# Column weights of the input and up projections kept as pairs in five slots, each starting at another byte offset modulo 512

## The chip, the cores and the metric

The kernel runs on one core of one Trainium2 chip. The metric is the device time of one execution in microseconds; lower is better. "TensorE", "VectorE", "ScalarE", "GpSimd" and "SyncE" are the core's engines; the profile calls them PE, DVE, ACT, POOL and SP, and lists TensorE's weight loads apart as PEld. SBUF is the on-chip memory with 128 partitions, PSUM holds the matmul results in 8 banks, DRAM is off-chip memory.

## The reference

One decoder layer over a sequence of 2048 positions with 1024 channels, in float32. Its parts, cut to what is computed:

```python
h = rms_norm(x, mix_norm_g[l])
z = h @ w_in[l]                                  # 1024 -> 2048: the input projection
lru_x, lru_gate, conf_a, conf_b = jnp.split(z, [D_LRU, 2 * D_LRU, 2 * D_LRU + D_CONF], axis=-1)
lru_x = causal_dwconv(lru_x, lru_conv_w[l], lru_conv_b[l])              # 4 taps
y_lru = rg_lru(lru_x, ...) * jax.nn.gelu(lru_gate, approximate=True)
c = conf_a * jax.nn.sigmoid(conf_b)
c = causal_dwconv(c, conf_conv_w[l], conf_conv_b[l])                    # 31 taps
c = jax.nn.silu(layer_norm(c, conf_ln_g[l], conf_ln_b[l]))
x = x + jnp.concatenate([y_lru, c], axis=-1) @ w_out[l]
...
x = x + o @ w_o[l]                               # cross-attention into 256 memory tokens
h = rms_norm(x, ffn_norm_g[l])
g, u = jnp.split(h @ w_up[l], 2, axis=-1)        # 1024 -> 6144: the up projection
g = causal_dwconv(g, ffn_conv_w[l], ffn_conv_b[l])                      # 3 taps
x = x + (jax.nn.gelu(g, approximate=True) * u) @ w_down[l]              # 3072 -> 1024
return rms_norm(x, final_norm_g)
```

## The kernel before

The kernel first records all its operations in a `Program`, and a planner then decides their order on each engine before anything is emitted. All operations are emitted in one place (line 394), so the profile tells them apart by tile names and not by lines.

**Precision.** A float32 product is made of three float32r products (TensorE's rounded float32): each operand is split into a high part, a rounded copy made by ScalarE, and a low part, source minus high part, made by VectorE (`split`, line 566). `mm3` then issues high x high, high x low and low x high into the same PSUM bank. The first operand of a matmul is the stationary one, 128x128, loaded into TensorE ahead of the matmul; the second one moves through it, mostly 512 columns wide.

**The two projections.** In the input projection (`project`) and the up projection (`strassen_cols`) the weights are the stationary operand. They come in blocks of 4 x 128 rows by 128 columns, each split into a high and a low tile of 128 x 512 elements, named wh and wl and made by `pair("w", (P, KQ, P))`. One such pair serves 12 matmuls: four 128-row steps, three products each.

- The input projection runs once per quarter of the sequence (four "mixers" of 512 positions). In the first mixer the weights are loaded raw, split, used, and stored to DRAM as w_in2 (`Columns.store`); the three later mixers load the stored parts again (`Columns.get`, `Kept.get`), 32 pairs each.
- The up projection runs once per half of the sequence, in 12 chunks of 256 gate and 256 value columns. Each of these column blocks is computed by Strassen's method with seven products per block pair; sums of raw blocks (tiles named s) are made by VectorE, split, and used once. That makes 2 x 12 x 2 x 7 = 336 pairs. The moving operands are seven sets of four split tiles (Xh, Xl), 56 tiles that stay in SBUF for a half. The tiles u, up, gb and cv take the PSUM results, their sums and the convolution with its gelu.
- While the up projection runs, `prepare_down` splits the combined blocks of w_down, also with pairs named wh and wl, but without the shape argument, and stores them for the down projection, where they are the moving operand.

**Slots.** Every working tile is one of a class: S (128 x 512, 84 slots), W (raw weights, 128 x 1024, 4 slots), D (128 x 1152, 3 slots) and ps (8 PSUM banks). Within a class the planner hands slots out strictly in the order in which the program created the tiles; a slot is free when the last operation on its tile has ended. S, W and D slots are 2048, 4096 and 4608 bytes per partition, all multiples of 512, and the first of them starts on a multiple of 512. The constants (identity matrix, ones) lie 128 bytes past one.

**Order.** `deadlines` gives each operation a due time, counted back from the order of TensorE's work, also through the slots (the operation that frees a slot is due before the one that needs it). `schedule` lets each engine take its ready operation with the nearest due time. The result is a fixed instruction order per engine; an instruction whose operands are not there holds up those behind it on its engine. All DMAs are issued by SyncE, in one such order. Stores have a slack of 30 us in their due times.

Of the kernel before, what the change touches and what calls it, by code (L numbers as in the profile page):

```python
# [12 lines left out]
F32R = mybir.dt.float32r  # L13
# [4 lines left out]
P = 128  # L18
S = 2048
D = 1024  # L20
NK = D // P
KQ = NK // 2
TT = 512
NQ = S // TT
NH = NQ // 2
NTB = TT // P
# [12 lines left out]

SLOTS = dict(S=84, W=4, D=3, ps=8)
WIDTH = dict(S=TT, W=1024, D=1152, ps=TT)


ACT_SETS = {AF.Exp: (0,), AF.Tanh: (0, 2, 11, 18), AF.Sigmoid: (2,), AF.Sqrt: (3,),
# [84 lines left out]
class Program:  # L131
# [3 lines left out]
    def __init__(self, nc, place):  # L135

        self.nc, self.place = nc, place
        self.ops, self.clock, self.group, self.queues = [], 0.0, None, {t: [] for t in SLOTS}
        self.first = False
        self.engines = dict(PE=nc.tensor, DVE=nc.vector, ACT=nc.scalar, Pool=nc.gpsimd, SP=nc.sync)  # L140

    def new(self, tag, shape=None, dtype=F32, name="t"):
        b = Buf(tag, shape or (P, WIDTH[tag]), None, dtype, name)
        self.queues[tag].append(b)
        return b
# [68 lines left out]
    def prepare(self):  # L214

        for tag, queue in self.queues.items():
            live = []
            for b in queue:
                while live and live[0] < b.ops[0].idx:
                    heapq.heappop(live)  # L220
                heapq.heappush(live, b.ops[-1].idx)
                assert len(live) <= SLOTS[tag], tag
        for o in self.ops:
# [3 lines left out]
        for tag, queue in self.queues.items():  # L227
            dead = sorted(queue, key=lambda b: b.ops[-1].idx)
            for i, b in enumerate(queue[SLOTS[tag]:]):
                for u in dead[i].ops:  # L230
# [24 lines left out]
    def schedule(self):  # L255
# [3 lines left out]
        idle = {e: True for e in self.engines}  # L259
        free = {t: list(range(n)) for t, n in SLOTS.items()}  # L260
        queues = {t: list(reversed(q)) for t, q in self.queues.items()}
# [13 lines left out]
        def grant(tag, t):  # L275
            while free[tag] and queues[tag]:
                b = queues[tag].pop()
                b.slot = free[tag].pop(0)
                b.left = len(b.ops)
                for o in b.heads:  # L280
                    satisfied(o, t)
# [62 lines left out]
        for tag, queue in self.queues.items():  # L344
            for b in queue:
                for o in b.heads:
                    o.wait += 1
        for tag in SLOTS:
            grant(tag, 0.0)
# [68 lines left out]
def hybrid_layer(  # L418
# [12 lines left out]

    def place(b, slot):
        pool = psp if b.tag == "ps" else spool
        return pool.tile([P, WIDTH[b.tag]], b.dtype, name=b.name, tag=f"{b.tag}{slot}", bufs=1)

    pr = Program(nc, place)

    def const(shape, name, dtype=F32):
        return Buf(None, shape, cpool.tile(list(shape), dtype, name=name), dtype, name)

    def V(name, *a, **k):
        pr.do("DVE", name, *a, **k)
# [20 lines left out]
    def tmp(name="tmp"):  # L463
        return pr.new("S", name=name)

    def rnd(name, shape=None):
        return pr.new("S", shape, F32R, name)

    def pair(name, shape=None):
        return rnd(name + "h", shape), rnd(name + "l", shape)  # L470


# [93 lines left out]
    def split(src, hi, lo):  # L566
        ACT(hi[:], src, AF.Copy)
        V("tensor_tensor", lo[:], src, hi[:].f32(), op=ALU.subtract)
# [13 lines left out]
    def load_gates():  # L582
        for name, w in (("gwa", lru_w_a), ("gwx", lru_w_x)):
            g = tmp()
            V("memset", g[:], 0.0)
            gr = g[:].split2(NC4)
            wr = w[0].rearrange("(c t) i j -> t i c j", t=2)
            for t in range(2):
                pr.dma(gr[t * 64 : t * 64 + 64, :, t * 64 : t * 64 + 64], wr[t])
            hi, lo = pair(name)  # L590
            split(g[:], hi, lo)
            gates.append((hi, lo))


    class Kept:
# [12 lines left out]
            self.tok[i] = Buf(None, (1,))  # L608
            pr.dma(self.at(i), src.f32(), writes=[self.tok[i]])

        def get(self, i, shape=None, name=None):
            b = pr.new("S", shape, self.dtype, name or self.name)
            pr.dma((b[:] if shape is None else flat(b)).f32(), self.at(i), reads=[self.tok[i]])
            return b

    def raw_cols(w, c0, kq):
        st = pr.new("W", (P, KQ, 2 * P), name="raw")
        pr.dma(st[:], w[kq * KQ * P : (kq + 1) * KQ * P, c0 : c0 + 2 * P].rearrange("(k p) f -> p k f", p=P))
        return st
# [6 lines left out]
    def split_cols(st, f):  # L626
        hi, lo = pair("w", (P, KQ, P))
        split(st[:, :, f * P : (f + 1) * P], hi, lo)
        return hi, lo

    def flat(b):
        return Ref(b, (lambda ap: ap.rearrange("p k f -> p (k f)"),), np.broadcast_to(np.int8(0), (P, TT)))

    class Columns:

# [5 lines left out]
        def get(self, c0, kq):  # L641
            key = (c0, kq)
            n = self.seen[key] = self.seen.get(key, 0) + 1
            base = ((c0 // (2 * P)) * 2 + kq) * 4
            if n > 1:
                return [tuple(self.kept.get(base + 2 * f + i, (P, KQ, P), "w" + "hl"[i]) for i in range(2)) for f in range(2)]
            st = self.early.pop(key, None) or raw_cols(self.w, c0, kq)
            got = self.rounded(c0, kq, st)
            if n < self.uses:
                self.store(c0, kq, got)  # L650
            return got
# [8 lines left out]
        def store(self, c0, kq, got):  # L660
            base = ((c0 // (2 * P)) * 2 + kq) * 4
            for f in range(2):
                for i in range(2):
                    self.kept.put(base + 2 * f + i, flat(got[f][i]))

    class Rows:
# [5 lines left out]
        def get(self, k, half):  # L672
            base = (k * 2 + half) * 2
            n = self.seen[k, half] = self.seen.get((k, half), 0) + 1
            if n > 1 or self.w is None:
                return tuple(self.kept.get(base + i, None, "w" + "hl"[i]) for i in range(2))
            st = tmp("raw")
            pr.dma(st[:], self.w[k * P : (k + 1) * P, half * TT : (half + 1) * TT])
            hi, lo = pair("w")
            split(st[:], hi, lo)  # L680
            if n < self.uses:
                self.kept.put(base, hi[:])
                self.kept.put(base + 1, lo[:])
            return hi, lo
# [38 lines left out]
    class Stats:  # L723
# [3 lines left out]
        def add(self, tb, half, src):  # L727
            i = half * NTB + tb
            ACT(junk[:], src, AF.Square, accum_out=self.ss[:, i : i + 1])
# [313 lines left out]
    x2_kept = Kept("x2", NQ * NTB * 2, F32)  # L1043
# [131 lines left out]
    def attend(q, ready):  # L1175
# [7 lines left out]
        def add(tb, half, p):  # L1183
            V("tensor_tensor", xs[tb][half][:], xs[tb][half][:], p[:], op=ALU.add)
            st.add(tb, half, xs[tb][half][:])

        yield from project_tokens(L + Y, W_out, add, None, ATT_PACE[q][0])
        del L, Y
        r = st.rstd()
# [232 lines left out]
    wd_kept = Kept("w_down2", NCK * 7 * KD * 2)  # L1422

    def wd_at(c, key, i):
        return ((c * 7 + ORDER.index(key)) * KD + i) * 2
# [29 lines left out]
    class Down:  # L1455
# [34 lines left out]
        def gather(self, c, n):  # L1490
            if (c, n) in self.ready:
                return self.ready.pop((c, n))
            akey, bkey = self.STEPS[n]
            L, R = [], []
            for i in range(KD):
                src = self.operand(c, akey, i)
                hi, lo = pair("hid")
                split(src[:], hi, lo)
                L.append((hi, lo))
                at = wd_at(c, bkey, i)  # L1500
                R.append(self.given[c, n][i] if (c, n) in self.given else (wd_kept.get(at, None, "wh"), wd_kept.get(at + 1, None, "wl")))
            self.R = R
            return L, R

# [13 lines left out]
        def add(self, banks, th, half):  # L1518
            for tb in range(NTB):
                at = (th, tb, half)  # L1520
                if at not in self.acc:
                    self.acc[at] = x2_kept.get(((2 * self.h + th) * NTB + tb) * 2 + half, None, "acc")
                t = self.acc[at]
                V("tensor_tensor", t[:], t[:], banks[tb][:], op=ALU.add)

# [110 lines left out]
    m, n, a = mixers, normeds, attends  # L1636
# [40 lines left out]
```

## Time and profile before

| | us |
|---|---|
| median of two timed runs | 2470.62 (2469.7 to 2471.55) |
| the profiled execution | 2470.41 |
| its span, first to last instruction | 2468.5 |
| TensorE busy in the span | 2450.5 |
| VectorE busy | 1825.8 |
| ScalarE busy | 1171.0 |

The stages follow each other roughly so: mixers with the preparation of the attention weights and the first attention quarters until about 800 us, the remaining attention until 1070 us, the up projection until about 2010 us, the down projection to the end. DMA moved 543.70 MB in the span, 220 GB/s in the mean.

How to read the rows that the prediction quotes: in rows of instruction groups stand line, engine, operation, output tile and input tiles with the buffer numbers left out, rows and columns, and shape, then the count; after the bar the group's busy time, the mean nanoseconds of one, and how long the engine sat idle before them, with what ended that. Rows of waits give who waited for whom, the total, the number and the longest, in us. Rows of windows give the stretch, its length, then each engine's busy time with its number of instructions in the order TensorE, weight loads, VectorE, ScalarE, GpSimd, then the granted clock, the DMA engines' busy share and GB/s. Rows of the timeline give start, duration, engine and instruction; equal ones that follow each other are merged with a count. Matmuls overlap in the pipeline, so a matmul's listed duration is longer than the distance to the next one.

### The profile page before, as it was taken

How to read it: one execution, taken by the hardware profiler on the slowest of the kernel's cores; microseconds unless marked ns; L12 is line 12 of the kernel's file. 1: busy time of each engine (PE TensorE's matmuls, PEld its weight loads, DVE VectorE, ACT ScalarE, POOL GpSimd, SP SyncE). 2: the span in 40 equal slices, each digit the busy share in tenths (PEclk: the TensorE clock that was granted, in tenths of full speed). 3: DMA queues.
4: the chain of work that ended last, by engine and by line, in shares of the span. 5: the costliest groups of instructions: out<-in, count | busy, mean ns of one | idle time of the engine just before them, and what ended most of it. 6: DMA issues, size and time to landing. Idle time of an engine off the chain costs nothing. (4 is left out here: it accounts for less than half of the span.)

```text
span 2468.5 us, 32772 instructions
## 1 busy us (share of the span) xinstructions
PE 2450.5 (99%) x11212; PEld 2037.8 (83%) x11212; DVE 1825.8 (74%) x3041; ACT 1171.0 (47%) x2041; POOL 0.7 (0%) x6
## 2 busy tenths in 40 slices
PE   9999999999999999999999999999999999999998
PEld 7898888888888788888888888888888888888887
DVE  7999993697279532369888887987886675667666
ACT  6762664366416543465545455555454432224223
POOL 0000000000000000000000000000000000000000
PEclk9999999999999999999999999999999999999999
DMA  9598676677456748777654545444542387779675
GB/s 318 209 302 320 214 256 236 214 257 257 150 174 238 250 158 293 260 254 249 234 196 151 181 165 178 166 165 163 179 145 94 120 279 263 247 253 357 234 253 177
DMA packets 327741, 543.70 MB, mean 220 GB/s; under 512 B 31580, under 2 KB 109404, under 8 KB 327574
## 3 DMA queue, kind: packets, MB, share of 16 engines
q1 hardware_dynamic: 327574, 541.60, 63.9%
q8 instruction: 89, 1.46, 0.2%
q14 instruction: 78, 0.64, 0.1%
HBM read 396.78 MB, written 144.70 MB: 219 GB/s over the span
## 5 line engine op out<-in xcount | busy, mean ns | idle before, releaser
L394 PE MATMUL ps<-Xh,wh 128*128 128x512 f32 x1344 | 523.4, 389 | 0.0
L394 PE MATMUL ps<-Xh,wl 128*128 128x512 f32 x1344 | 523.0, 389 | 0.1
L394 PE MATMUL ps<-Xl,wh 128*128 128x512 f32 x1344 | 522.9, 389 | 0.0
L394 DVE SCALAR_TENSOR_TENSOR conv<-cb,v,conv 128x512 f32<-128x512 f32 x480 | 339.6, 743 | 2.8 <-ACT conv L394 0.9
L394 PEld LDWEIGHTS ps<-Xh,wl 128*128 128x128 f32 x1344 | 252.2, 188 | 53.2 <-DVE wl L394 0.6
L394 PEld LDWEIGHTS ps<-Xh,wh 128*128 128x128 f32 x1344 | 252.3, 188 | 52.7 <-DVE up L394 0.4
L394 PEld LDWEIGHTS ps<-Xl,wh 128*128 128x128 f32 x1344 | 252.3, 188 | 52.2
L394 PE MATMUL ps<-wl,hidh 128*128 128x512 f32 x672 | 261.4, 389 | 0.0
L394 PE MATMUL ps<-wh,hidh 128*128 128x512 f32 x672 | 261.4, 389 | 0.0
L394 PE MATMUL ps<-wh,hidl 128*128 128x512 f32 x672 | 261.4, 389 | 0.0
L394 DVE TENSOR_TENSOR acc<-acc,ps 128x512 f32<-128x512 f32 x192 | 129.4, 684 | 143.8 <-PE ps L394 141.2
L394 PE MATMUL ps<-xh,wh 128*128 128x512 f32 x512 | 202.7, 396 | 0.8 <-ACT xt L394 0.8
L394 PE MATMUL ps<-xh,wl 128*128 128x512 f32 x512 | 199.4, 389 | 0.0
L394 PE MATMUL ps<-xl,wh 128*128 128x512 f32 x512 | 199.3, 389 | 0.0
L394 ACT ACTIVATE wh<-s 128x512 fp32r<-128x512 f32 x192 | 119.3, 627 | 111.9 <-DVE s L394 85.6
L394 ACT ACTIVATE wh<-raw 128x512 fp32r<-128x512 f32 x208 | 127.1, 626 | 85.0 <-PE ps L394 40.1
L394 DVE TENSOR_TENSOR wl<-raw,wh 128x512 fp32r<-128x512 f32 x208 | 141.0, 684 | 24.6 <-ACT wh L394 22.9
L394 DVE TENSOR_TENSOR wl<-s,wh 128x512 fp32r<-128x512 f32 x192 | 131.1, 686 | 29.0 <-ACT wh L394 20.2
L394 ACT ACTIVATE u<-ps 128x512 f32<-128x512 f32 x144 | 85.9, 597 | 138.9 <-PE ps L394 137.9
L394 PEld LDWEIGHTS ps<-wh,hidh 128*128 128x128 f32 x672 | 126.1, 188 | 26.2
L394 PEld LDWEIGHTS ps<-wl,hidh 128*128 128x128 f32 x672 | 126.1, 188 | 26.2
L394 PEld LDWEIGHTS ps<-wh,hidl 128*128 128x128 f32 x672 | 126.1, 188 | 26.1
(206 smaller groups left out, 4246.0 us busy)
## 6 DMA issues: line engine op xcount, KB each, us to landing
raw<-in_w_up_dram SPq DMA_DIRECT2D x96, 512.0 KB
wh<-w_down SPq DMA_DIRECT2D x164, 256.0 KB
wl<-w_down SPq DMA_DIRECT2D x164, 256.0 KB
wh<-w_in SPq DMA_DIRECT2D x96, 256.0 KB
wl<-w_in SPq DMA_DIRECT2D x96, 256.0 KB
hid<-cv SPq DMA_DIRECT2D x48, 512.0 KB
h<-hid SPq DMA_DIRECT2D x96, 256.0 KB
w_down<-wh SPq DMA_DIRECT2D x84, 256.0 KB
```

The costliest lines, as they stand in the source:

```text
L394: getattr(e, name)(*[resolve(a) for a in args], **{k: resolve(a) for k, a in kw.items()})
```

## The change

Pairs with a shape argument, that is the column weights of the input and up projections, get a class T of their own: one tile of 128 x 1024 elements with the high part in its first half and the low part in its second. T has five slots of 4608 bytes per partition (1024 + 128 elements of 4 bytes). Within slot n the pair starts `T_AT[n]` elements from the slot's start: 0, 192, 64, 128 and 32 bytes for the slots 0 to 4. The class S goes from 84 to 74 slots. `Kept.get_pair` loads the two stored parts with two DMAs into the halves of one T tile; `join` marks the second as not waiting for the first. The other hunks of the diff only drop an argument from the calls of `Kept.get`.

```diff
-SLOTS = dict(S=84, W=4, D=3, ps=8)
-WIDTH = dict(S=TT, W=1024, D=1152, ps=TT)
+SLOTS = dict(S=74, T=5, W=4, D=3, ps=8)
+WIDTH = dict(S=TT, T=1024, W=1024, D=1152, ps=TT)
+T_PAD, T_AT = 128, [0, 48, 16, 32, 8]
...
     def place(b, slot):
         pool = psp if b.tag == "ps" else spool
+        if b.tag == "T":
+            t = pool.tile([P, WIDTH["T"] + T_PAD], b.dtype, name=b.name, tag=f"T{slot}", bufs=1)
+            return t[:, T_AT[slot] : T_AT[slot] + WIDTH["T"]]
         return pool.tile([P, WIDTH[b.tag]], b.dtype, name=b.name, tag=f"{b.tag}{slot}", bufs=1)
...
     def pair(name, shape=None):
+        if shape is not None:
+            t = pr.new("T", (P, 2 * KQ, P), F32R, name)
+            return t[:, :KQ], t[:, KQ:]
         return rnd(name + "h", shape), rnd(name + "l", shape)
...
-        def get(self, i, shape=None, name=None):
-            b = pr.new("S", shape, self.dtype, name or self.name)
-            pr.dma((b[:] if shape is None else flat(b)).f32(), self.at(i), reads=[self.tok[i]])
+        def get(self, i, name=None):
+            b = pr.new("S", None, self.dtype, name or self.name)
+            pr.dma(b[:].f32(), self.at(i), reads=[self.tok[i]])
             return b
+
+        def get_pair(self, i, name):
+            got = pair(name, (P, KQ, P))
+            for n, b in enumerate(got):
+                pr.dma(flat(b).f32(), self.at(i + n), reads=[self.tok[i + n]], join=n > 0)
+            return got
...
     def flat(b):
-        return Ref(b, (lambda ap: ap.rearrange("p k f -> p (k f)"),), np.broadcast_to(np.int8(0), (P, TT)))
+        return Ref(b.buf, b.steps + (lambda ap: ap.rearrange("p k f -> p (k f)"),), np.broadcast_to(np.int8(0), (P, TT)))
...
             if n > 1:
-                return [tuple(self.kept.get(base + 2 * f + i, (P, KQ, P), "w" + "hl"[i]) for i in range(2)) for f in range(2)]
+                return [self.kept.get_pair(base + 2 * f, "w") for f in range(2)]
```

More of the change, by code (lines that the diff above doesn't have):

```diff
@@ L675, in get @@
             if n > 1 or self.w is None:
-                return tuple(self.kept.get(base + i, None, "w" + "hl"[i]) for i in range(2))
+                return tuple(self.kept.get(base + i, "w" + "hl"[i]) for i in range(2))
             st = tmp("raw")
@@ L1500, in gather @@
                 at = wd_at(c, bkey, i)
-                R.append(self.given[c, n][i] if (c, n) in self.given else (wd_kept.get(at, None, "wh"), wd_kept.get(at + 1, None, "wl")))
+                R.append(self.given[c, n][i] if (c, n) in self.given else (wd_kept.get(at, "wh"), wd_kept.get(at + 1, "wl")))
             self.R = R
@@ L1521, in add @@
                 if at not in self.acc:
-                    self.acc[at] = x2_kept.get(((2 * self.h + th) * NTB + tb) * 2 + half, None, "acc")
+                    self.acc[at] = x2_kept.get(((2 * self.h + th) * NTB + tb) * 2 + half, "acc")
                 t = self.acc[at]
```

## The prediction

> **What bounds the kernel now.** I read the page first, then instructions grouped by line and shape, then the waits, then busy time by windows.
>
> ```profile
> span 2468.5 us, 32772 instructions
> PE 2450.5 (99%) x11212; PEld 2037.8 (83%) x11212; DVE 1825.8 (74%) x3041; ACT 1171.0 (47%) x2041; POOL 0.7 (0%) x6
> PEclk9999999999999999999999999999999999999999
> ```
>
> TensorE is busy from end to end at the full granted clock. The profiled execution took 2470.41 us (1.91 us around its span), the two timed runs have a median of 2470.62; the sum below is made against 2470.4. "Busy" alone could hide gaps, because each matmul is listed longer than the distance to the next. So I look at what TensorE waited for, largest first, and the last of the ten rows:
>
> ```profile
> PE ps L394 <- DMA raw<-in_ffn_norm_g_dram: 3.3, 1, 3.3
> PE ps L394 <- ACT mem L394: 2.0, 1, 2.0
> PE ps L394 <- DVE sum L394: 1.7, 1, 1.7
> ...
> PE ps L394 <- DVE xl L394: 0.3, 1, 0.3
> ```
>
> Nothing of note. Hence the time is the number of matmuls times the distance between them, and only two things can move it: that distance, or new waits. The distance comes from a window that holds nothing but 512-column matmuls of the up projection:
>
> ```profile
> 1600.00:2000.00 400.00, 400.00 (x1766) 331.23 (x1765) 305.85 (x463) 188.03 (x286) 0.00 (x0) 1.00 0.43 147
> ```
>
> 400/1766 = 226.5 ns each, although one is listed at 389 ns and its weight load at 188 ns in the rows that follow. What does the distance consist of? The matmuls of 256 columns tell, also in rounded float32 (float32r), each with a fresh 128x128 weight load:
>
> ```profile
> 128.70 0.28 PE L394 MATMUL ps<-kvl,qth 128*128 128x256 f32 x1
> ...
> 130.38 0.28 PE L394 MATMUL ps<-kvh,qth 128*128 128x256 f32 x1
> ```
>
> These are 14 steps in 1.68 us, 120 ns each. So 256 more columns cost 106.5 ns (0.416 ns a column), and 120 - 256 x 0.416 = 13.5 ns remain per matmul, whatever its length. This constant is the only thing that the byte shift can remove.
>
> **What the shift touches.** The matmuls whose stationary operand moves into the new slots are these six groups, three of the up and three of the input projection:
>
> ```profile
> L394 PE MATMUL ps<-Xh,wh 128*128 128x512 f32 x1344 | 523.4, 389 | 0.0
> L394 PE MATMUL ps<-Xh,wl 128*128 128x512 f32 x1344 | 523.0, 389 | 0.1
> L394 PE MATMUL ps<-Xl,wh 128*128 128x512 f32 x1344 | 522.9, 389 | 0.0
> L394 PE MATMUL ps<-xh,wh 128*128 128x512 f32 x512 | 202.7, 396 | 0.8 <-ACT xt L394 0.8
> L394 PE MATMUL ps<-xh,wl 128*128 128x512 f32 x512 | 199.4, 389 | 0.0
> L394 PE MATMUL ps<-xl,wh 128*128 128x512 f32 x512 | 199.3, 389 | 0.0
> ```
>
> 3 x (1344 + 512) = 5568 matmuls, 12 to a pair, so 464 pairs. By the changed program's order the unshifted slot serves 95 of them; 369 pairs, 4428 matmuls, read their weights 32, 64, 128 or 192 bytes off. Every slot of the old program holds a multiple of 512 bytes, and weights and moving operand of all its float32r matmuls start at the same place modulo 512. So no row of before shows a float32r matmul with a shift. Bounds: at best the whole constant goes, 4428 x 13.5 ns = 59.8 us. At worst I have no row; the weight load may grow from 188 ns by 38 ns before it reaches the distance of 226.5.
>
> Which value? The nearest rows are plain float32. The identity matrix starts 128 bytes off a multiple of 512, the tile x on one:
>
> ```profile
> 7.56 1.91 PE L394 MATMUL ps<-ident,x 128*128 128x128 f32 x16
> 9.30 1.91 PE L394 MATMUL ps<-ident 128*128 128x128 f32 x16
> ```
>
> Sixteen transposes with operands 128 bytes apart and sixteen of the identity with itself (no distance at all) take the same 1.91 us. The weight load shows no price either: in `sum,ones` the stationary matrix lies 128 bytes off, in `mt,raw` on a multiple:
>
> ```profile
> L394 PEld LDWEIGHTS ps<-mt,raw 128*128 128x128 f32 x256 | 48.3, 190 | 8.2 <-DVE al L394 1.2 <-issue 0.5
> L394 PEld LDWEIGHTS ps<-sum,ones 128*128 128x128 f32 x16 | 3.0, 190 | 2.7 <-DVE sum L394 2.1
> L394 PEld LDWEIGHTS ps<-Xl,wh 128*128 128x128 f32 x1344 | 252.3, 188 | 52.2
> ```
>
> 190 and 190 ns. I take 0 for the shift, gain and loss, and keep the ends. A second reason against a clash of two reads: once one stream has been held up by a step it no longer meets the other, so a clash should not return for every load with the same 13.5 ns at 256 and 512 columns. A constant does. The Trainium skill (TensorE: Matmul & The Clock Gate, "Step-by-step: what each phase is for") states that TensorE has two independent read ports, one for the moving operand and one for weight loads, so that a load takes no read bandwidth from the running matmul. By that rule the shift is worth nothing, and the sum stays as it is. The same page's "Back-to-back issue gap" gives 2.5 ns above the column time for a warm matmul. The trace shows 13.5 ns for float32r, so the page's figure does not hold here, and what fills the difference is open.
>
> **What the slots cost.** Before, a pair took any two of 84 general slots; now it needs one of five. A slot is free when the last of its 12 matmuls has run and, in the first mixer, when both its stores to DRAM have landed. With five slots in turn, a refill has four products of time: 4 x 12 x 226.5 ns = 10.9 us. The refill itself is one copy and one subtraction:
>
> ```profile
> L394 ACT ACTIVATE wh<-s 128x512 fp32r<-128x512 f32 x192 | 119.3, 627 | 111.9 <-DVE s L394 85.6
> L394 DVE TENSOR_TENSOR wl<-s,wh 128x512 fp32r<-128x512 f32 x192 | 131.1, 686 | 29.0 <-ACT wh L394 20.2
> ```
>
> 0.63 + 0.69 = 1.3 us, which leaves 9.6 us for what stands ahead in the two queues. Behind a refill that waits for its slot stand ScalarE's PSUM copies (u) and VectorE's additions into gb and up, for which TensorE's banks wait. The longest single instructions there are:
>
> ```profile
> L394 DVE SCALAR_TENSOR_TENSOR cv<-gb,v,cv 128x1024 f32<-128x1024 f32 x40 | 51.2, 1280 | 5.3 <-ACT cv L394 3.4 <-DMA wd<-in_w_down_dram 1.3
> L394 DVE TENSOR_TENSOR cv<-cv,up 128x512 f32<-128x512 f32 x40 | 27.4, 685 | 0.4
> L394 ACT ACTIVATE cv<-gb,v 128x1024 f32<-128x1024 f32 x20 | 24.8, 1238 | 14.9 <-DVE gb L394 14.7
> ```
>
> In the changed order nine of the 459 refills have less time: two come one product after the release (2.7 us), seven two products (5.4 us). One instruction ahead in each queue makes a refill 1.3 + 1.24 + 1.28 = 3.8 us: the two are late by 1.1 us each, the seven are not. Price 2 us, between 0 and 10 us if all nine were late by that much.
>
> The first mixer splits 32 pairs and stores each (0.52 MB):
>
> ```profile
> 0.00:100.00 100.00, 94.70 (x461) 79.96 (x462) 81.60 (x169) 68.28 (x121) 0.70 (x6) 1.00 0.87 304
> 700.00:800.00 100.00, 99.16 (x453) 82.02 (x452) 99.54 (x169) 44.39 (x68) 0.00 (x0) 1.00 0.59 202
> ```
>
> At 304 GB/s a pair's store takes 1.7 us, within refill distances of 9.7 to 14 us there. DMA engines are 87% busy, so some will land late: I take 2 us, up to 13 if each of 26 refills is late by 0.5. The later mixers load 96 pairs by DMA; the tightest stretch is at 737 to 750 us with 10.9 us from release to use, and at 202 GB/s (the row above) 0.52 MB takes 2.6 us. These two DMAs now wait at SP for TensorE's release, with x, xn and w_out loads behind them. SP waits in this way already:
>
> ```profile
> SPq L394 <- PE ps L394: 623.2, 330, 30.1
> ```
>
> No TensorE wait came of it, so 0. The number and size of DMAs stay the same. The 74 general slots hold 56 tiles of split activations during the up projection, which leaves 18 instead of 28, but the ten are those that the pairs used: 0. The down projection gets ten slots less and none back; its program-order peak is 56 of 74: 0.
>
> Sum: 2470.4 + 0 (shift) + 2 + 2 = 2474.4, so 2474.
>
> **Rivals.**
>
> The shift works (faster). If the 13.5 ns are two reads at the same place modulo 512, the four shifted slots lose it in whole or in part: 2474.4 - 59.8 = 2415 in whole, and about 2456 if three tenths go. For it: the constant is there, and all float32r operands do start at the same place. Against it: the transposes above, and a constant independent of length. Chance 0.12 in all, 0.03 of it for the 83% of the constant that make 2%.
>
> VectorE's burst empties the five slots (slower). Its place is the convolution of each of 24 chunks in the up projection: four cv steps and four products, 4 x 1.28 + 4 x 0.685 = 7.9 us of VectorE. Run in one piece, that is under the 9.6 us of cover; it decides from 9.6 on. Two additions into gb (0.69 each) and two s sums on top make 10.7, late by 1.1 us a chunk; with two more of each, 13.4, late by 3.8. Over 24 chunks that is 26 to 91 us; at 2.4 late it is 58 us, 2532. For it: VectorE was 93% busy at 1100 to 1200 us and 89% at 1500 to 1600:
>
> ```profile
> 1100.00:1200.00 100.00, 99.84 (x449) 82.07 (x448) 92.91 (x151) 59.77 (x94) 0.00 (x0) 1.00 0.71 245
> 1500.00:1600.00 100.00, 100.00 (x443) 82.81 (x442) 88.96 (x143) 56.42 (x92) 0.00 (x0) 1.00 0.52 179
> ```
>
> Against it: the planner puts the instruction with the nearest due time first, a split before a convolution step, and between 1600 and 2000 us VectorE has 94 of 400 us to spare. Chance 0.06.
>
> The shift hurts: each nanosecond of distance costs 4.4 us, 11 of them 2%. Nothing shows it; chance 0.02. That the change doesn't do what it says is excluded: a slot is 4608 bytes, nine times 512, so the starts do differ as written.
>
> **How the numbers follow.** Forecast 2474, chance 0.80, between 2468 and 2494 by the bounds above (10 and 13 us of lateness at the upper end). The range takes in a small relief down to 2458 (2.8 ns of the constant, 12 us off 2470.4). Left out are most of the relief case (0.10) and the two slow ones (0.08). About 2% can be told from no change, 49 us: faster 0.03, slower 0.05 (the burst beyond 49 us, and the shift's own price), the rest within.
>
> **What would show it.** Matmuls per microsecond in a window of the up projection: still 4.4 if the shift does nothing, up to 4.7 if it removes the constant. In the same window TensorE's distance would differ from pair to pair, by slot. TensorE's waits on wl (now w) growing from under 1 us to a few says that the slots cost what I priced; tens of microseconds there, at chunk boundaries, is the burst. I am wrong if the distance moves in either direction, or if waits appear outside the nine short refills and the first 100 us.

## The result and the profile after

The changed kernel takes 2505.18 us (median of two runs, 2504.64 to 2505.71), the one before 2470.62: a ratio of 1.014 with a 95% interval of 1.0096 to 1.0183. It is 34.6 us slower, outside the predicted range of 2458 to 2494, and by more than the runs scatter. The profiled execution took 2504.64 us with a span of 2502.9, which is 34.4 more than before. All operations now stand at line 395, as the diff adds a line above.

The page's head after, with busy time and count of each engine:

```profile
span 2502.9 us, 32672 instructions
PE 2479.1 (99%) x11212; PEld 2038.9 (81%) x11212; DVE 1829.3 (73%) x3041; ACT 1177.1 (47%) x2044; POOL 0.7 (0%) x6
PEclk9999999999999999999999999999999999999999
```

The count of matmuls, the time of all weight loads (2037.8 before) and the granted clock are all but the same, and TensorE is still busy from end to end. Its busy time grew by 28.6 us. The same window of the up projection as in the prediction:

```profile
1600.00:2000.00 400.00, 400.00 (x1728) 324.25 (x1727) 311.25 (x471) 187.36 (x284) 0.00 (x0) 1.00 0.41 142
```

1728 matmuls where 1766 were: 400/1728 = 231.5 ns from one to the next instead of 226.5, at full clock and without a gap. Does the whole kernel run slower, or only what reads the new slots? The groups by form after, in the columns of the prediction, first those with a pair, then those of the down projection, which uses none, then a weight load from a pair:

```profile
L395 PE MATMUL ps<-Xh,w 128*128 128x512 f32 x2688 | 841.4, 394 | 2.7 <-DVE w L395 0.9 <-ACT u L395 0.7 <-ACT Xh L395 0.6
L395 PE MATMUL ps<-Xl,w 128*128 128x512 f32 x1344 | 528.7, 393 | 0.2 <-DVE Xl L395 0.2
L395 PE MATMUL ps<-wh,hidh 128*128 128x512 f32 x672 | 261.5, 389 | 0.8 <-ACT hidh L395 0.8
L395 PE MATMUL ps<-wl,hidh 128*128 128x512 f32 x672 | 261.4, 389 | 0.0
...
L395 PEld LDWEIGHTS ps<-Xh,w 128*128 128x128 f32 x2688 | 504.7, 188 | 121.3 <-DVE w L395 1.9 <-ACT u L395 1.3 <-ACT Xh L395 1.0
```

Of these rows only the matmuls with a pair are longer (394 and 393 against 389 ns); the loads from it are listed at 188 ns as before. So what slows are the matmuls, and the load's own row doesn't show it. The waits of TensorE, largest first, are the smaller part:

```profile
PE ps L395 <- DMA raw<-in_ffn_norm_g_dram: 3.5, 1, 3.5
PE ps L395 <- ACT xt L395: 2.2, 2, 1.3
PE ps L395 <- ACT xh L395: 1.7, 1, 1.7
...
PE ps L395 <- DVE w L395: 0.9, 1, 0.9
```

The 34.4 us can be divided by the distances between the starts of successive matmuls in the two traces, each put beside the 226.75 ns (120 ns at 256 columns) of the kernel before. Steps that touch a shifted operand are longer by 23.5 us in sum (4530 steps), steps just behind them and other unshifted ones by 1.7 more than before, gaps (what steps of 300 ns and more have above that distance) grew from 12.0 to 22.1 us, and the rest is 0.9 us less.

### The profile page after: what moved, and what is told of

It reads as the page before. It is cut to its first block, busy times and chain, and to the rows that moved or that the text cites. A ratio compares the mean times of both kernels' runs of the same rounds, so it can differ in the third digit from the quotient of the medians.

```text
span 2502.9 us, 32672 instructions
## 1 busy us (share of the span) xinstructions
PE 2479.1 (99%) x11212; PEld 2038.9 (81%) x11212; DVE 1829.3 (73%) x3041; ACT 1177.1 (47%) x2044; POOL 0.7 (0%) x6
## 4 chain that ended last, share of the span: by engine, by line
PE 64%; DMA 1%; DVE 1%; ACT 1%; issue 0%; SPq 0%; ACTq 0%; DVEq 0%
PE ps L395 64%; DMA wl<-w_down 1%; DMA out_dram<-acc 0%; ACT Xh L395 0%; DVE conv L395 0%; ACT xn L395 0%; DVE r L395 0%; ACT w L395 0%; ACT prob L395 0%; DVE ptl L395 0%; DVE s L395 0%; DVE gate L395 0%; DVE hidl L395 0%; ACT pth L395 0%; DVE acc L395 0%
## 5 line engine op out<-in xcount | busy, mean ns | idle before, releaser
L395 PE MATMUL ps<-Xh,w 128*128 128x512 f32 x2688 | 841.4, 394 | 2.7 <-DVE w L395 0.9
L395 PEld LDWEIGHTS ps<-Xh,w 128*128 128x128 f32 x2688 | 504.7, 188 | 121.3 <-DVE w L395 1.9
L395 PE MATMUL ps<-Xl,w 128*128 128x512 f32 x1344 | 528.7, 393 | 0.2 <-DVE Xl L395 0.2
L395 PE MATMUL ps<-xh,w 128*128 128x512 f32 x1024 | 334.0, 396 | 0.8 <-ACT xt L395 0.8
L395 PEld LDWEIGHTS ps<-Xl,w 128*128 128x128 f32 x1344 | 252.6, 188 | 58.4 <-DVE Xl L395 0.5
L395 PEld LDWEIGHTS ps<-xh,w 128*128 128x128 f32 x1024 | 192.4, 188 | 45.0 <-ACT xt L395 1.1
L395 ACT ACTIVATE w<-s 128x512 fp32r<-128x512 f32 x192 | 120.5, 630 | 176.8 <-PE ps L395 156.9
L395 PE MATMUL ps<-xl,w 128*128 128x512 f32 x512 | 201.5, 394 | 0.0
L395 DVE TENSOR_TENSOR w<-raw,w 128x512 fp32r<-128x512 f32 x176 | 120.6, 688 | 67.4 <-ACT w L395 66.9
L395 DVE TENSOR_TENSOR w<-s,w 128x512 fp32r<-128x512 f32 x192 | 131.2, 687 | 2.5 <-ACT w L395 2.0
```

The source lines that it names most:

```text
L395: getattr(e, name)(*[resolve(a) for a in args], **{k: resolve(a) for k, a in kw.items()})
```

## The experiments

Each starts from the changed kernel, except where the text names the kernel before. The kernel before ran beside them on the same chip, at 2470.0 to 2470.3 us.

**No shift.**

```diff
-T_PAD, T_AT = 128, [0, 48, 16, 32, 8]
+T_PAD, T_AT = 128, [0, 0, 0, 0, 0]
```

> All five slots start on a multiple of 512 bytes; the class with five slots and everything else stay as in the change. Theory A (the shift lengthens the distance between matmuls, and the slots add waits): the 23.5 us that stand above 226.75 ns in the changed kernel's 4530 matmul steps with a shifted operand go, the 10.1 us of longer gaps stay: about 2481 us, distance in the up projection 226.5 to 227 ns. Rival B (the longer distance comes from the pairs being one tile in five slots, whatever their address, for instance an additional wait on the whole tile): 2505 us, distance stays at 229 to 236 ns.

2484.46 us, ratio 1.0058 (1.0043 to 1.0073). Theory A holds in its main part: the distance is back, as the window of the up projection shows,

```profile
1600.00:2000.00 400.00, 400.00 (x1766) 331.24 (x1765) 310.03 (x474) 188.74 (x290) 0.00 (x0) 1.00 0.45 152
```

and 5057 steps inside pairs take 226.8 ns in the mean. What stays, 14.3 us, goes with the slots: gaps sum to 27.7 us, 5.6 more than in the changed kernel. Of these 5.6, 3.1 us are 17 steps in two stretches of 3.4 us, at 531 and 2282 us, in which the granted clock was half; the trace of the changed kernel has no such stretch between its first and last 10 us. That the rest grew because faster matmuls leave ScalarE and VectorE less time is not shown: without the half-rate steps, gaps sum to 24.6 us here, but, counted the same way, to 22.4 us in another kernel with the short distance (all pairs at 256 bytes, below), against 22.1 in the changed kernel. Taking the shift away is worth 20.7 us net; 14.3 us are left for the slots.

**One shift for all.**

```diff
-T_PAD, T_AT = 128, [0, 48, 16, 32, 8]
+T_PAD, T_AT = 128, [16, 16, 16, 16, 16]
```

> All five slots start 64 bytes past a multiple of 512. Theory A1 (the price hangs on where the weights lie against the moving operand): the 5568 matmuls all show what the 64-byte slot showed, 233.4 ns, 6.7 ns more each: 2481 + 37 = 2518 us. Rival A2 (the price comes from changing between slots of different shifts): with one shift the distance falls back to 227 ns, about 2481 us.

2517.72 us, ratio 1.0195 (1.0179 to 1.021), as A1 has it. 5057 steps inside pairs take 233.4 ns in the mean. The price is steady and does not come from changing between slots:

```profile
1600.00:2000.00 400.00, 400.00 (x1716) 320.58 (x1715) 312.56 (x473) 188.00 (x285) 0.00 (x0) 1.00 0.42 144
```

**Everything moved, and the other operand moved.** In the first kernel 64 bytes of padding among the constants move all working tiles of the kernel before; in the second 448 bytes of padding with 64 bytes in the slots put the pairs on a multiple of 512 and everything else 64 bytes below one.

```diff
-    smalls = cpool.tile([P, 488], F32, name="smalls")
+    smalls = cpool.tile([P, 504], F32, name="smalls")    # kernel before
...
-    smalls = cpool.tile([P, 488], F32, name="smalls")
+    smalls = cpool.tile([P, 600], F32, name="smalls")    # changed kernel
+T_PAD, T_AT = 128, [16, 16, 16, 16, 16]
```

> The kernel before with 64 bytes of padding among its constants, so that every working tile, stationary and moving alike, starts 64 bytes past a multiple of 512. Theory R (only the distance between the two operands modulo 512 counts): 2470.6 us and 226.5 to 227 ns, as before. Rival P (the place of the weights against a multiple of 512 counts by itself): some 9900 float32r matmuls of 512 columns at 6.7 ns more: about 2537 us.

2471.30 us, ratio 1.0006 (0.9997 to 1.0016): no difference from before, and 1766 matmuls in the window:

```profile
1600.00:2000.00 400.00, 400.00 (x1766) 331.22 (x1765) 306.14 (x463) 188.85 (x286) 0.00 (x0) 1.00 0.44 147
```

> Pairs on a multiple of 512 bytes, and every other working tile, the moving operands among them, 64 bytes below one; the distance between the operands is the same 64 bytes as with all five slots shifted by 64. Theory R: the same time as that kernel, about 2518 us. Rival P: weights on a multiple of 512 cost nothing, but the down and output projections, whose operands are both off, pay: 2481 + 4700 x 0.0067 = about 2512 us if being off costs them 6.7 ns each, with the up projection at 227 ns; the distance in the up projection tells the two apart, 233 against 227 ns.

2516.98 us, ratio 1.0189 (1.0172 to 1.0206), the time of all pairs shifted by 64, and the same window count:

```profile
1600.00:2000.00 400.00, 400.00 (x1716) 322.30 (x1715) 312.79 (x471) 187.76 (x284) 0.00 (x0) 1.00 0.43 144
```

Theory R holds: moving both operands by 64 bytes costs nothing. What counts is how far apart, in this measure, the weights and the moving operand lie.

**Other shifts.**

```diff
+T_PAD, T_AT = 128, [64, 80, 96, 112, 4]       # 256, 320, 384, 448, 16 bytes
...
+T_PAD, T_AT = 128, [1, 2, 40, 120, 124]       # 4, 8, 160, 480, 496 bytes
```

> Five other shifts: 256, 320, 384, 448 and 16 bytes. Theory C (zero is the best place, any other distance makes the two reads meet): every slot shows 228 to 236 ns; 5568 matmuls at some 6 ns on top of the 2484 us of the unshifted slots, about 2517 us. Rival D (the 13.5 ns constant is itself such a meeting, and some distance avoids it): at least one slot falls clearly below 226 ns, down to 213 ns; each ns over one slot's 1114 matmuls is worth 1.1 us.

> Shifts of 4, 8, 160, 480 and 496 bytes. Theory C: the shifts below 16 bytes either act like zero (227 ns, if the place counts in steps of 16 bytes or more) or cost as the others do; 480 is 32 bytes below a multiple and costs what 32 does, 233 ns; about 2510 us. Rival D: a slot below 226 ns.

One execution each: 2500.65 and 2508.41 us. The distance inside a pair (start to start, some 1000 steps a slot, gaps of 280 ns and more left out) from these two traces, the changed kernel's and those with one shift:

| shift in bytes | ns |
|---|---|
| 0 and 256, one shift for all | 226.8, 226.8 |
| 16, 496 | 227.4, 227.2 |
| 4, 8 | 232.2, 230.9 |
| 32, 480 | 233.1, 233.2 |
| 64, 320 | 233.4, 233.5 |
| 128, 384 | 232.5, 232.9 |
| 160 | 233.6 |
| 192, 448 | 229.4, 229.5 |

Rival D falls: no slot is below 226 ns in the mean. Theory C holds in that none is better than zero, but not in that all others cost: 16 bytes up or down cost at most 0.6 ns, and 256 next to nothing. In the mixture the 256-byte slot showed 228.5 ns, but its last steps in a pair stood at 226.7. So the question was whether the shift repeats with 256 bytes.

```diff
-T_PAD, T_AT = 128, [0, 48, 16, 32, 8]
+T_PAD, T_AT = 128, [64, 64, 64, 64, 64]
```

> All five slots 256 bytes past a multiple of 512. Theory Q (the price repeats every 256 bytes, and what the 256-byte slot showed among others was left over from its neighbours): distance 226.5 to 227 ns and the time of the unshifted kernel, 2484 us. Rival: 256 bytes cost the 1.8 ns that the slot showed in the mixture, 5568 x 1.8 = 10 us more, 2494 us.

2483.14 us, ratio 1.0052 (1.0037 to 1.0067): the time of the unshifted kernel, 226.8 ns over 5048 steps.

```profile
1600.00:2000.00 400.00, 400.00 (x1767) 331.20 (x1766) 310.02 (x473) 188.63 (x289) 0.00 (x0) 1.00 0.45 151
```

**Where the slots' 14 us come from.** First the number of pair slots, unshifted, at the memory of the kernel before:

```diff
-SLOTS = dict(S=74, T=5, W=4, D=3, ps=8)
+SLOTS = dict(S=72, T=6, W=4, D=3, ps=8)       # and S=76, T=4 in the other
-T_PAD, T_AT = 128, [0, 48, 16, 32, 8]
+T_PAD, T_AT = 0, [0] * 6                     # [0] * 4 in the other
```

> Unshifted pairs, six slots for them and 72 general ones (five and 74 in the unshifted kernel at 2484.5 us). Theory L (the added waits come from too few pair slots, that is too little time to refill): they shrink, 2475 to 2480 us. Rival M (they come from the general slots that were given away, of which the attention and the down projection have the use): they grow, 2488 to 2495 us, with more gaps in stages that use no pair, at 800 to 1000 us and above 2010 us.

> Unshifted pairs, four slots for them and 76 general ones. Theory L: the waits grow, as a refill has three products, 8.2 us, instead of four: 2490 to 2520 us, the new gaps in the mixers and in the up projection. Rival M: they shrink a little, 2478 to 2483 us.

2484.70 us (ratio 1.0057, 1.0040 to 1.0074) and 2484.30 us (1.0057, 1.0042 to 1.0072). Four, five or six pair slots give the same time, which neither theory had expected. But each pair slot more is two general ones less, and equal times can hide two effects that cancel. The windows from 500 to 600 us, in a mixer that loads its pairs by DMA, say that they partly do; with five, six and four slots:

```profile
500.00:600.00 100.00, 97.32 (x433) 79.00 (x432) 96.90 (x166) 60.88 (x81) 0.00 (x0) 0.98 0.75 258
```

```profile
500.00:600.00 100.00, 100.00 (x456) 82.09 (x455) 99.55 (x170) 61.86 (x82) 0.00 (x0) 1.00 0.78 269
```

```profile
500.00:600.00 100.00, 99.09 (x449) 80.77 (x448) 97.28 (x167) 54.08 (x76) 0.00 (x0) 1.00 0.77 264
```

TensorE is idle here for 2.7, 0.0 and 0.9 us, and between 2010 and 2440 us, in the down projection, for 1.4, 2.3 and 2.2 us. Neither follows the number of pair slots in one direction. So the lookahead that I had priced, product by product, does not set the time by itself, and these two runs don't part it from the number of general slots. Next, the pair as two separate tiles:

```diff
-SLOTS = dict(S=74, T=5, W=4, D=3, ps=8)
+SLOTS = dict(S=74, T=10, W=4, D=3, ps=8)
-WIDTH = dict(S=TT, T=1024, W=1024, D=1152, ps=TT)
+WIDTH = dict(S=TT, T=TT, W=1024, D=1152, ps=TT)
...
+            return tuple(pr.new("T", shape, F32R, name + i)[:] for i in "hl")
```

> Unshifted pairs as two tiles each again, high and low apart, in ten slots of their own beside 74 general ones; the memory is that of the kernel before. Theory O (the 14 us of the unshifted kernel come from a pair being one tile, so that its first matmul waits for the low part too and both halves are freed together): they go, 2470 to 2473 us. Rival N (they come from dividing one pool of slots in two): they stay, 2480 to 2488 us.

2483.12 us, ratio 1.0053 (1.0036 to 1.0069): the single tile is not the cause, and the waits remain with the division of the pool. Last, the kernel before with its one pool made smaller:

```diff
-SLOTS = dict(S=84, W=4, D=3, ps=8)
+SLOTS = dict(S=82, W=4, D=3, ps=8)            # and S=79 in the other
```

> The kernel before with 82 general slots instead of 84, nothing else. Rival P (any other slot count gives the planner another order, and the order of before was the lucky one): several us more at once, 2475 to 2484 us. Theory N (capacity counts): two slots are little, 2470 to 2473 us.

> The kernel before with 79 general slots. Theory N (capacity counts): the time grows step by step, 2473 to 2480 us, more than with 82. Rival P: no order between 84, 82 and 79; 79 may be faster than 82.

2471.12 us (ratio 1.0005, 0.9995 to 1.0014) and 2488.54 us (1.0072, 1.0057 to 1.0087). Two slots less cost nothing that can be told, five cost 18.6 us, more than expected. So the pool of before had hardly any slack. Where are the slots missed? Three stretches show idle time. The start of the up projection, in the kernels before, unshifted, with two tiles, and with 79 slots:

```profile
1070.00:1200.00 130.00, 129.84 (x587) 107.07 (x586) 110.85 (x181) 80.54 (x133) 0.00 (x0) 1.00 0.67 231
```

```profile
1070.00:1200.00 130.00, 125.51 (x561) 101.82 (x561) 108.34 (x179) 79.05 (x136) 0.00 (x0) 1.00 0.73 255
```

```profile
1070.00:1200.00 130.00, 125.41 (x560) 101.70 (x560) 108.19 (x179) 79.73 (x134) 0.00 (x0) 1.00 0.74 253
```

```profile
1070.00:1200.00 130.00, 125.62 (x555) 103.09 (x554) 104.18 (x172) 77.24 (x132) 0.00 (x0) 0.97 0.67 229
```

The last three have some 4 us of idle TensorE that the first does not have, and 26 to 32 matmuls less. With 82 slots the kernel before is idle here for 1.1 us, so that 84, 82 and 79 slots stand in order. Here the 56 tiles of split activations are made while pairs, sums and PSUM copies already need slots. The second stretch is the down projection, which uses no pair and had only lost slots. Of the unshifted kernel's timeline (start, duration, in brackets the idle time and what ended it):

```profile
2278.62 0.39 PE L395 MATMUL ps<-wl,hidh 128*128 128x512 f32 x1
2279.18 0.49 PE L395 MATMUL ps<-wh,hidl 128*128 128x512 f32 x1 [0.17 <-DVE hidl L395]
2280.45 0.50 PE L395 MATMUL ps<-wh,hidh 128*128 128x512 f32 x1 [0.77 <-ACT hidh L395]
...
2281.59 0.50 PE L395 MATMUL ps<-wh,hidl 128*128 128x512 f32 x1 [0.41 <-DVE hidl L395]
...
2283.30 0.63 PE L395 MATMUL ps<-wl,hidh 128*128 128x512 f32 x1
2283.72 0.63 PE L395 MATMUL ps<-wh,hidl 128*128 128x512 f32 x1
2284.15 0.63 PE L395 MATMUL ps<-wh,hidh 128*128 128x512 f32 x1
```

TensorE waits for split hidden tiles, and after the waits it runs seven steps at about 427 ns. The window tells why: the granted clock is 0.79 in these 8 us and 1.00 in the next.

```profile
2278.00:2286.00 8.00, 6.65 (x20) 4.50 (x19) 8.00 (x14) 3.68 (x6) 0.00 (x0) 0.79 1.05 395
2286.00:2294.00 8.00, 8.00 (x37) 6.59 (x36) 5.62 (x10) 1.34 (x3) 0.00 (x0) 1.00 0.96 332
```

So this cluster of waits cost its idle time, and matmuls at half rate followed. They need not follow: with all pairs at 256 bytes the same three waits (0.17, 0.76 and 0.42 us) stand at the same place, and the clock stays full:

```profile
2278.00:2286.00 8.00, 6.64 (x28) 4.61 (x27) 8.00 (x14) 3.69 (x6) 0.00 (x0) 1.00 1.03 389
```

What decides between the two is open. The third stretch lies at 529 us, where the unshifted kernel waits 1.86 and 0.82 us for the split input of the gates (xh and xl), in a stage that takes 32 pairs by DMA. This one is not a matter of general slots alone: with 79 slots and no class of pairs, TensorE has no idle time between 500 and 600 us. Together the three stretches have 8.4 us more idle time than the kernel before (4.3, 1.4 and 2.7), and the 17 half-rate steps add 3.1 us; where the rest of the 14.3 us arises is not shown.

## Why the prediction was wrong

**That only the distance or new waits could move the time** was right, and it was both.

**The shift at 0.** This is the step that failed: "I take 0 for the shift, gain and loss". It cost 23.5 us in the trace, 5.3 ns for each of 4428 matmuls, and 20.7 us net. The slots alone, with 2484.5 us, would have stayed inside the range. Both reasons behind the 0 were weak. The transposes are plain float32 with another matmul form, and their equal 1.91 us said nothing of float32r at 128 bytes, which costs 5.7 ns. That the load's row keeps its length (190 and 190 ns then, 188 and 188 now) says nothing of the matmuls, and it was the wrong row to look at. The bound upward was drawn from it too ("the weight load may grow from 188 ns by 38 ns"), whereas the price came without any growth of the load. And the argument that two streams no longer meet after one hold-up gave no ground for the 0 either, as the price is steady: with one shift of 64 bytes the steps inside pairs stay at 230 to 236 ns for the whole kernel. I had a price list (4.4 us per ns) and gave its upper side 0.02.

The Trainium skill (TensorE: Matmul & The Clock Gate, "Step-by-step: what each phase is for") has two independent read ports, so that a load takes no read bandwidth from the running matmul. By that rule the place of the weights would be worth nothing. The trace does not agree: with the loads' length unchanged, their place against the moving operand alone is worth up to 6.8 ns a matmul, and the measurement decides. That the load and the running matmul hinder each other is not shown by it. In the kernel with one shift of 64 bytes, the step beside the first shifted load behind unshifted ones still takes 227.1 ns (mean of 49), and the step that ends a shifted stretch, beside an unshifted load, takes 230.0 ns (mean of 48). The Trainium skill (SBUF — State Buffer, "Door 1: The DMA port swizzle") puts SBUF's lines at 16 bytes. The table agrees in part only: 16 bytes either way cost at most 0.6 ns, and 4 and 8 bytes cost 5.4 and 4.1, but 32 bytes, which are whole lines too, cost 6.3.

**The slots at 4 us.** Right in kind, wrong in size and place: 14.3 us without the shift, 10.1 us of gaps with it. I counted short refills, and the time did not follow the number of pair slots (2484.5, 2484.7 and 2484.3 us for five, six and four). What I set at 0, "the ten are those that the pairs used" and the down projection's spare room, was a large part of the cost: of the idle time that is new in the unshifted kernel, 4.3 us stand at the start of the up projection, where the undivided pool with 79 slots has as much, and 1.4 in the down projection. The count of tiles live in program order (56 of 74 in the down projection) told only that the program fits, not how far the planner runs ahead with what is spare.

**The rivals.** The shift that works did not occur. The burst of VectorE at every chunk did not either: between 1600 and 2000 us the unshifted kernel loses nothing. The shift that hurts is what happened, at 5.3 instead of the 11 ns that would make 2%.

What stays open: why the distance depends on the two places, and with a period of 256 bytes, as far as four pairs of shifts show it (0 and 256, 64 and 320, 128 and 384, 192 and 448), and what the 13.5 ns constant at zero shift is. It was not removed by any of the 14 shifts tried. That the missing slots act through capacity and not through a less fortunate order of the planner is supported by the order 84, 82, 79 (2470, 2471, 2488 us) and by idle time in two of the three stretches. But a planner given more than 84 slots was not tried, though the slots of the changed kernel take 2560 bytes per partition more than those of the kernel before, which is room for an 85th.

## What to carry to other kernels

Keep the stationary and the moving operand of float32r matmuls at the same place modulo 256 bytes, as tiles of a multiple of 512 bytes do by themselves; padding one of them by 32 to 192 bytes costs 3 to 7 ns of 227 per matmul, and no row of the weight loads shows it. Read the distance from matmul to matmul by counting starts in a full window, not from the listed duration. A reserved class of slots in a full pool can cost the stages that cannot use it: before dividing a pool, run the old kernel with as many slots less.

## What had not been expected of the hardware

- The distance between float32r matmuls of 512 columns hangs on the difference of their operands' addresses, 226.8 ns at 0 and 256 bytes, up to 233.6 ns at others, whichever operand is moved.
- The steps alternate with the products: in the one kernel with the slot at 320 bytes they take 231 and 236 ns by turns, at 448 bytes 226, 229 and 232.
- Three waits within 3 us, 1.35 us of idle time in sum, were followed by seven steps at half rate (427 ns) and a granted clock of 0.79 over 8 us; the same three waits in the kernel with all pairs at 256 bytes were followed by a full clock.
